# Five small edits to a two-block transformer kernel: zero products, modulation sums, a reordered norm, a join, low parts

## The chip, the cores and the metric

The kernel runs on one core of one Trainium2 chip. The time is that of one execution on the device, in microseconds (us); the number to compare is the median of several runs.

## The reference, cut to what matters

Two blocks of two layers each run over 512 tokens with 1024 features, one after the other, all in fp32.

```
for layer in range(2):                                # first block
    sh1, sc1, g1, sh2, sc2, g2 = split(silu(c) @ ada_w[layer] + ada_b[layer], 6)
    h = rms_norm(x, norm_mix_g[layer]) * (1 + sc1) + sh1
    mix = (RG-LRU and stick-breaking attention)(h) if layer == 0 else (sliding window, sinks)(h)
    x = x + g1 * mix
    h = rms_norm(x, norm_ffn_g[layer]) * (1 + sc2) + sh2
    x = x + g2 * conv_ffn(h)
for layer in range(2):                                # second block
    if layer == 0:
        x = x + diff_attention(rms_norm(x, a_norm)) @ a_w_o
    else:
        k, v = split(rms_norm(x, kv_norm) @ kv_w)     # three groups of 16 heads
        q = rms_norm(x, b_norm) @ b_w_q
        o, lse = [attention with dilation 1, 4, 16 for each group]
        x = x + sum(softmax(lse) * o) @ b_w_o
    x = x + square(relu(rms_norm(x, m_norm[layer]) @ m_w_up[layer])) @ m_w_down[layer]
```

The six modulation vectors of a layer come from one product of a vector with a 1024x6144 matrix. In the dilated attention a query of the group with dilation 4 or 16 sees tokens that lie 4 or 16 apart.

## The kernel before

The residual `x` lies in SBUF with features on partitions: eight chunks `xs[k]` of 128 features by 512 tokens. Every weight product is made of three fp32r products: weights and activations are each split into a high part (a cast) and a low part (the value less its high part), and high x high, low x high and high x low are added up in PSUM. So a chunk of normalised activations takes three steps: the scaled value `t` on VectorE, its high part on ScalarE, its low part on VectorE. A product of a unit takes all eight chunks.

The program isn't written in the order in which it runs. Generators yield operations to a list scheduler (`Flow`) that keeps a clock of its own, has a queue with priorities for each engine, and lets an operation go when its engine is free in the model and its inputs are there. `P_LO` (-1) stands ahead of `P_SECOND` and `P_CRIT` (0), and these ahead of the attention (`P_ATT`, 5). The outcome is one fixed order of instructions for each engine. Buffers are counted in pools ("a": 33 large ones of 4 KB a partition, "t": 14 temporaries); a task waits until it is granted one.

The places that the change touches:

- `layer0_in`, the start. The first chunks come by DMA with their weights; the modulation of layer 0 is made on TensorE in between. Six PSUM banks hold the sums of the first weights. Since two halves of a bank are summed in turn, each bank is first set to zero by a product with a tile of zeros `z` (a memset on GpSimd), as the first thing on TensorE.
- `ada_finish`, the modulation of layer 1. VectorE makes partial sums in the background (`ada_fold`, into `adap`); when a segment is complete, four small products with `sel4` collect the sums of 32 partitions, on TensorE, with the priority `P_CRIT`. It happens three times.
- `h_chunk` makes the normalised chunk of one half of the tokens (256 each), `h_perm` the same for the dilated layer with tokens in another order. The low part of the second half has `P_SECOND`, the one of the first half `P_LO`.
- `layer3`, the dilated attention. For its group 0 the tokens lie in the order "b r j" (blocks of 128, inside them by the remainder r of 4), made in `in3`; groups 1 and 2 need the order "r b j" over all tokens. `second` makes these chunks (`x2`) with `h_perm` after the last unit of group 0, and the buffers of the old order (`x`) come free when all units of group 0 are through. `units` runs a product in two passes of 256 tokens, each pass with two tiles of 128 tokens over all eight chunks.
- `join` adds the weighted outputs of two groups and writes them in the order "b r j"; so the product with `b_w_o` comes out in that order, and `residual` adds it to `xs` through a view that goes through the tokens in steps of four (`perm`).

Of the kernel before, what the change touches and what calls it, by code (L numbers as in the profile page):

```python
# [16 lines left out]
P = 128  # L17
# [191 lines left out]
def body(ctx, tc, I, out, upto=8):  # L209
# [25 lines left out]
    def tmp(n=S):  # L235
        return mk("t", (P, n))
# [106 lines left out]
    one1 = const("one1", (P, 1))  # L343
    adap = const("adap", (P, 192))
# [180 lines left out]

    def proj_tm(u, x, tpair, kinds=()):
        ps = yield from getps(*kinds)
        for t in range(2):
            o = ps[:, t * 256 : (t + 1) * 256]
            tok = slice((2 * tpair + t) * P, (2 * tpair + t + 1) * P)  # L530
            for k in range(8):
                yield x.ready[k][tpair]
                hh, hl = x.h(k)[:, tok], x.l(k)[:, tok]
                wh, wl = u.w(k, slice(0, 256))
                yield mm(3 * fr(256), (o, hh, wh, k == 0, False), (o, hh, wl, False, False), (o, hl, wh, False, k == 7))
        return ps
# [51 lines left out]
    def h_chunk(x, k, hf, r, g, sh=None):  # L588
# [5 lines left out]
        if sh is None:  # L594
            yield acopy(hi, t)
            yield tt(lo, t, hi.bitcast(F32), ALU.subtract, prio=P_SECOND if hf else P_LO)
        else:
            yield act(hi, t, AF.Identity, bias=sh[:, k : k + 1])
            yield stt(lo, t, sh[:, k : k + 1], hi.bitcast(F32), ALU.add, ALU.subtract, prio=P_SECOND if hf else P_LO)
# [158 lines left out]
    def ada_finish(l, segs):  # L758
        s0, n = segs[0], 8 * len(segs)
        if l == 0:  # L760
# [4 lines left out]
            return  # L765
        yield ("pt", 1)
# [225 lines left out]
    def setup():  # L992
# [6 lines left out]
        yield vcopy(silu32[:, :, 0:1], silu_c.unsqueeze(2))  # L999

# [91 lines left out]
    def layer0_in():  # L1092
# [43 lines left out]
        yield ("t", 1)  # L1136
        z = tmp()
        G.memset(z, 0.0)
        for kind in ("pj", "pj", "pj", "ps", "ps", "po"):
            ps = yield from getps(kind)  # L1140
            pss.append(ps)

            yield mm(f4(S), (ps, z[:, :P], z, True, False))
        put("t")
        for k in range(KC):
            yield fr[k]
            yield x.ready[k][0]
            hi, lo = fw[k]
            for m in range(3):
# [485 lines left out]
    def h_perm(x, k, order, ready, h0=0, h1=2):  # L1635
# [10 lines left out]
        yield tt(x.l(k)[:, sl], t, x.h(k)[:, sl].bitcast(F32), ALU.subtract, prio=P_SECOND if h0 else P_LO)  # L1646
# [14 lines left out]
    def layer3(x, tabs):  # L1661
# [102 lines left out]
        def join(o0, o1, y, c, fin):  # L1764
# [3 lines left out]
            yield tt(ta.rearrange("p (b r j) -> p b r j", b=4, r=4), o0[:, c].rearrange("p (b r j) -> p b r j", b=4, r=4),  # L1768
# [38 lines left out]
        for hq in range(4):  # L1807
            three = unit(0, hq, "k"), unit(0, hq, "q"), unit(0, hq, "v")
            k, q, v = yield from (units(x, *three) if hq == 0 else singly(x, three))
# [6 lines left out]
        x.free()  # L1816
        put("rp", 4)
        x2_begun = spawn(second(), P_CRIT)
# [4 lines left out]
        for hq in range(4):  # L1823
            o0, md0, p0, e0 = pre0[hq]
            t = []
            for g in (1, 2):
                for e in tab1 + tab2 * (g - 1):
                    yield e
                k = yield from units(x, unit(g, hq, "k"))
# [10 lines left out]
        yield from out_quarters("bwo", ys, made, perm=True)  # L1840
# [254 lines left out]
```

## Time and profile before

| | us |
|---|---|
| median of 3 runs (2805.18 to 2805.73) | 2805.64 |
| the profiled execution | 2801.65 |
| its span, first to last instruction | 2799.9 |
| TensorE busy (matmul) | 2735.3 |
| VectorE busy | 1777.9 |
| ScalarE busy | 1239.8 |

The span is 1.75 us shorter than the execution that it belongs to. TensorE is near to always busy, so the time is the sum of its products at the clock granted, and of its waits. Line numbers (L304) are those of helpers: every product has L304, every transpose L310, VectorE's tensor_tensor L262, scalar_tensor_tensor L265, ScalarE's activation L292 and copy L295. Names are those of tile pools: a large buffers, t temporaries, b PSUM banks, x the residual.

### The profile page before, as it was taken

What the parts mean: (1) busy time and instruction counts of PE and PEld (TensorE: products, weight loads), DVE (VectorE), ACT (ScalarE), POOL (GpSimd) and SP (SyncE); (2) the same over time, 40 slices, a digit from 0 to 9 for tenths busy, and PEclk for the clock granted to TensorE, in tenths of its full rate; (3) what the DMA queues carried; (4) which work ended last, traced back from release to release, by engine and by line L of the source; (5) the groups of instructions that cost most, each with busy time, mean ns of one, the idle gap of its engine ahead of it and who ended that gap; (6) DMA issues with size and microseconds to landing.
All of it is one profiled execution on the core that took longest, in us unless ns stands there. A gap on an engine that the chain in (4) does not pass through costs nothing.

```text
span 2799.9 us, 43737 instructions
## 1 busy us (share of the span) xinstructions
PE 2735.3 (98%) x17298; PEld 2381.3 (85%) x17298; DVE 1777.9 (63%) x4114; ACT 1239.8 (44%) x2634; POOL 6.4 (0%) x57
## 2 busy tenths in 40 slices
PE   9999999999989999999999999999999999899999
PEld 7777987889869888899988888889899999788888
DVE  5678986457886444588795333676767767943333
ACT  4684423235744232356553322466656554433221
POOL 0000000000000000000000000000000000000000
PEclk9999999999989999999999999999999999999999
DMA  8335564331112223221222223221112123122331
GB/s 306 103 136 218 190 227 148 103 108 61 62 53 91 90 99 112 91 76 46 84 75 84 98 93 103 99 76 61 65 65 76 60 70 97 63 76 91 105 105 62
DMA packets 80270, 281.90 MB, mean 101 GB/s; under 512 B 8896, under 2 KB 11712, under 8 KB 80064
## 3 DMA queue, kind: packets, MB, share of 16 engines
q1 hardware_dynamic: 80064, 279.10, 29.6%
q8 instruction: 136, 2.23, 0.3%
q14 instruction: 70, 0.57, 0.1%
HBM read 276.97 MB, written 2.10 MB: 100 GB/s over the span
## 4 chain that ended last, share of the span: by engine, by line
PE 87%; DVE 9%; ACT 2%; issue 1%; DMA 1%; SPq 0%; ACTq 0%; DVEq 0%
PE b L304 83%; PE b L310 4%; DVE t L262 2%; DVE t L265 2%; DVE a L262 2%; DVE x L262 1%; DVE x L265 1%; DVE a L265 1%; ACT t L292 1%; DMA a<-in_ada_dram 1%; ACT a L295 0%; ACT L220 0%; DVE t L270 0%; DVE s L262 0%; ACT t L295 0%
## 5 line engine op out<-in xcount | busy, mean ns | idle before, releaser
L304 PE MATMUL b<-a,a 128*128 128x256 f32 (+3 forms) x15024 | 2549.0, 332 | 28.8 <-DVE a L262 14.1
L304 PEld LDWEIGHTS b<-a,a 128*128 128x128 f32 (+1 forms) x15024 | 2199.9, 191 | 316.3 <-issue 38.1
L295 ACT CAST a<-a 128x1024 fp32r<-128x1024 f32 (+2 forms) x354 | 357.0, 1035 | 324.5 <-DVE a L262 199.7
L262 DVE TENSOR_TENSOR a<-a,a 128x1024 fp32r<-128x1024 f32 (+2 forms) x362 | 428.8, 1196 | 28.3 <-ACT a L295 20.1
L292 ACT ACTIVATE t<-b 128x512 f32<-128x512 f32 x150 | 88.9, 598 | 313.7 <-PE b L304 312.6
L262 DVE TENSOR_TENSOR x<-b,x 128x512 f32<-128x512 f32 (+1 forms) x144 | 81.8, 573 | 204.2 <-PE b L304 203.6
L295 ACT COPY t<-b 128x512 f32<-128x512 f32 (+3 forms) x194 | 101.2, 524 | 214.9 <-PE b L304 148.0
L265 DVE SCALAR_TENSOR_TENSOR x<-b,mod,x 128x256 f32<-128x256 f32 (+1 forms) x176 | 104.5, 604 | 114.9 <-PE b L304 114.6
L265 DVE SCALAR_TENSOR_TENSOR a<-a,vec,a 128x256 fp32r<-128x256 f32 x288 | 133.1, 483 | 39.4 <-ACT a L292 38.9
L310 PE MATMUL b<-ident,t 128*128 128x128 f32 x896 | 141.3, 278 | 7.6 <-ACT t L295 2.6
L273 DVE CAST a<-t 128x512 fp32r<-128x512 f32 x64 | 27.4, 428 | 190.4 <-ACT t L292 190.4
L295 ACT COPY a<-b 128x512 f32<-128x512 f32 (+1 forms) x146 | 78.1, 537 | 145.1 <-PE b L304 95.9
L292 ACT ACTIVATE a<-a,vec 128x256 fp32r<-128x256 f32 x288 | 132.1, 501 | 0.6 <-DMA a<-in_kvw_dram 0.4
L310 PEld LDWEIGHTS b<-ident,t 128*128 128x128 f32 x896 | 103.0, 141 | 34.0 <-issue 14.1
L292 ACT ACTIVATE t<-t,s,s 128x256 f32<-128x256 f32 (+3 forms) x192 | 113.4, 593 | 28.4 <-DVE s L265 28.4
L292 ACT ACTIVATE t<-t 128x512 f32<-128x512 f32 x108 | 67.6, 633 | 122.7 <-DVE t L265 121.0
L262 DVE TENSOR_TENSOR t<-t,t 128x256 f32<-128x256 f32 (+5 forms) x201 | 105.3, 530 | 13.8 <-ACT t L292 12.2
L276 DVE TENSOR_REDUCE s<-t 128x8 f32<-128x512 f32 (+1 forms) x84 | 56.7, 675 | 85.5 <-ACT t L292 84.9
L262 DVE TENSOR_TENSOR a<-t,a 128x512 fp32r<-128x512 f32 (+1 forms) x188 | 108.0, 601 | 4.2 <-ACT a L295 1.1
L292 ACT ACTIVATE t<-x 128x256 f32<-128x256 f32 (+1 forms) x120 | 51.5, 431 | 118.5 <-DVE x L265 57.1
L295 ACT CAST a<-t 128x256 fp32r<-128x256 f32 (+1 forms) x124 | 62.6, 510 | 90.4 <-DVE t L262 82.5
L262 DVE TENSOR_TENSOR t<-b,rp 128x256 f32<-128x256 f32 x256 | 94.0, 417 | 0.0
(111 smaller groups left out, 1401.7 us busy)
## 6 DMA issues: line engine op xcount, KB each, us to landing
a<-in_ada_dram SPq DMA_DIRECT2D x96, 512.0 KB, 5.3
a<-in_gu_dram SPq DMA_DIRECT2D x88, 512.0 KB, 4.5
a<-in_mu_dram SPq DMA_DIRECT2D x64, 512.0 KB, 4.1
a<-in_md_dram SPq DMA_DIRECT2D x64, 512.0 KB, 3.8
a<-in_kvw_dram SPq DMA_DIRECT2D x48, 512.0 KB, 3.9
a<-in_dn_dram SPq DMA_DIRECT2D x44, 512.0 KB, 3.8
a<-in_aqkv_dram SPq DMA_DIRECT2D x24, 512.0 KB, 4.0
a<-in_bwq_dram SPq DMA_DIRECT2D x24, 512.0 KB, 4.0
```

The lines of the kernel that those rows point to most:

```text
L262: return Op("V", ve(size(o)), lambda: V.tensor_tensor(o, a, b, op), prio=prio)
L265: return Op("V", ve(size(o)) + ptr(sc), lambda: V.scalar_tensor_tensor(o, a, sc, b, op0, op1), prio=prio)
L273: return Op("V", ve(size(o), fast), lambda: V.tensor_copy(o, a))
L276: return Op("V", ve(size(a)), lambda: V.tensor_reduce(o, a, AX.X, ALU.add))
L292: return Op("A", c, lambda: A.activation(o, a, f, scale=scale, **kw), tab=SET_OF.get(f.name), prio=prio)
L295: return Op("A", 0.83e-3 * size(o) + 0.07, lambda: A.copy(o, a), prio=prio)
L304: T.matmul(o, l, r, start=st, stop=sp)
L310: T.transpose(o, a, ident)
```

## The change

1. Start: the zero products become products of fp32r with a constant tile of zeros `zr`, and stand right ahead of the first chunk's products.
2. `ada_finish` waits for 15 us of the scheduler's clock before the sums of layer 1 are collected.
3. The last unit of group 0 (v) and the first one of the new order (k) go chunk by chunk over both passes (`units_k`), on banks that a zero product has set; the v unit gives back the old chunks two at a time, and `second` begins ahead of it.
4. `join` writes in the order of time, and the residual of `b_w_o` is added plainly.
5. The low part of a second half has the priority `P_LO`, too.

```diff
+    zr = const("zr", (P, P), F32R)
...
+    def zeros(ps, r):
+        return mm(fr(S), (ps, zr, r, True, False))
+
+    def units_k(x, u, release=False):
+        yield from u.begin()
+        w = yield from take(u.key)
+        pss = []
+        for tp in range(2):
+            pss.append((yield from getps(*ANY)))
+        for k in range(8):
+            for tp in range(2):
+                yield x.ready[k][tp]
+                if k == 0:
+                    yield zeros(pss[tp], x.h(0))
+                for t in range(2):
+                    o = pss[tp][:, t * 256 : (t + 1) * 256]
+                    tok = slice((2 * tp + t) * P, (2 * tp + t + 1) * P)
+                    hh, hl = x.h(k)[:, tok], x.l(k)[:, tok]
+                    wh, wl = w.w(k, slice(0, 256))
+                    yield mm(3 * fr(256), (o, hh, wh, False, False), (o, hh, wl, False, False), (o, hl, wh, False, k == 7 and t == 1))
+            if release and k % 2:
+                put("a", 2)
+        w.free()
+        for tp in range(2):
+            spawn(u.fin(pss[tp], tp), P_FIN)
+        return u.dst
...
-            yield tt(lo, t, hi.bitcast(F32), ALU.subtract, prio=P_SECOND if hf else P_LO)
+            yield tt(lo, t, hi.bitcast(F32), ALU.subtract, prio=P_LO)
...
+        late = ev()
+        fl.at(fl.now + 15.0, late.set)
+        yield late
         yield ("pt", 1)
         ps = bank()
         yield mm(1.0, *[(ps[:, :n], sel4[:, i, :], adap[...
...
+        yield ts(zr, ones, 0.0, None, ALU.mult)
...
-        yield ("t", 1)
-        z = tmp()
-        G.memset(z, 0.0)
         for kind in ("pj", "pj", "pj", "ps", "ps", "po"):
-            ps = yield from getps(kind)
-            pss.append(ps)
-            yield mm(f4(S), (ps, z[:, :P], z, True, False))
-        put("t")
+            pss.append((yield from getps(kind)))
         for k in range(KC):
             yield fr[k]
             yield x.ready[k][0]
             hi, lo = fw[k]
+            if k == 0:
+                for ps in pss:
+                    yield zeros(ps, hi[:, :S])
...
-            yield tt(ta.rearrange("p (b r j) -> p b r j", b=4, r=4), o0[:, c].rearrange("p (b r j) -> p b r j", b=4, r=4),
+            yield tt(ta.rearrange("p (b j r) -> p b r j", b=4, r=4), o0[:, c].rearrange("p (b r j) -> p b r j", b=4, r=4),
                      o1[:, c].rearrange("p (r b j) -> p b r j", b=4, r=4), ALU.add)
...
-            k, q, v = yield from (units(x, *three) if hq == 0 else singly(x, three))
+            if hq < 3:
+                k, q, v = yield from (units(x, *three) if hq == 0 else singly(x, three))
+            else:
+                k, q = yield from singly(x, three[:2])
+                x2_begun = spawn(second(), P_CRIT)
+                v = yield from units_k(x, three[2], True)
...
-        x.free()
         put("rp", 4)
-        x2_begun = spawn(second(), P_CRIT)
...
-                k = yield from units(x, unit(g, hq, "k"))
+                k = yield from (units_k if g == 1 and hq == 0 else units)(x, unit(g, hq, "k"))
...
-        yield from out_quarters("bwo", ys, made, perm=True)
+        yield from out_quarters("bwo", ys, made)
```

TensorE, the start of the program, before: the zero products (t_113 is the tile of zeros; b_115 to b_162 are the six banks), the first modulation products (with silu), a norm's sum (ones), and the first product of the first chunk (a_125, a_105).

```order
L304 MATMUL b_115<-t_113 128x512
L304 MATMUL b_143<-t_113 128x512
L304 MATMUL b_145<-t_113 128x512
L304 MATMUL b_150<-t_113 128x512
L304 MATMUL b_153<-t_113 128x512
L304 MATMUL b_162<-t_113 128x512
L304 MATMUL b_194<-a_131,silu_88 32x256 x4
...
L304 MATMUL b_262<-a_138,silu_88 32x256 x4
L304 MATMUL b_115<-a_125,a_105 128x256
```

The same engine and place in the changed kernel (b_114 to b_119 are the banks, a_128 and a_106 the first chunk).

```order
L304 MATMUL b_188<-a_134,silu_88 32x256 x4
...
L304 MATMUL b_256<-a_141,silu_88 32x256 x4
L304 MATMUL b_114<-a_128,zr 128x512
L304 MATMUL b_115<-a_128,zr 128x512
L304 MATMUL b_116<-a_128,zr 128x512
L304 MATMUL b_117<-a_128,zr 128x512
L304 MATMUL b_118<-a_128,zr 128x512
L304 MATMUL b_256<-one_89,t_270 128x1 x2
L304 MATMUL b_119<-a_128,zr 128x512
L304 MATMUL b_114<-a_128,a_106 128x256
```

The six zero products have moved from the head of the row to the first product that needs them.

TensorE in the feed-forward of layer 0, before: the third group of modulation sums (adap, sel) behind the last products of one weight unit.

```order
L304 MATMUL b_4395<-a_2592,a_4243 128x512
L304 MATMUL b_4395<-a_2591,a_4244 128x512
L304 MATMUL b_4444<-adap,sel_85 128x16 x4
L304 MATMUL b_4445<-a_2585,a_4230 128x512
L304 MATMUL b_4445<-a_2586,a_4230 128x512
```

In the changed kernel the row behind that unit (b_4394) is at once a product (b_4443), and the sums stand in a later unit.

```order
L304 MATMUL b_4394<-a_2592,a_4245 128x512
L304 MATMUL b_4394<-a_2591,a_4246 128x512
L304 MATMUL b_4443<-a_2585,a_4220 128x512
...
L304 MATMUL b_4548<-a_2585,a_4404 128x512
L304 MATMUL b_4563<-adap,sel_85 128x16 x4
L304 MATMUL b_4548<-a_2585,a_4403 128x512
```

The sums have moved from row 2132 of TensorE's order to row 2207; all rows between are products of 128x512.

VectorE at the change of token order, before: the last small operation of a norm (s_19324), low parts of weights (with vec), and then the chunks in the new order (t<-x,rstd, four-dimensional views) with their low parts.

```order
L269 TENSOR_SCALAR s_19324<-s_19324 128x8
L265 SCALAR_TENSOR_TENSOR a_19335<-a_19333,vec,a_19334 128x256
L265 SCALAR_TENSOR_TENSOR a_19331<-a_19329,vec,a_19330 128x256
...
L262 TENSOR_TENSOR t_19495<-x,rstd 128x4x4x32
L262 TENSOR_TENSOR t_19497<-x,rstd 128x4x4x32
L262 TENSOR_TENSOR t_19498<-x,rstd 128x4x4x32
L262 TENSOR_TENSOR a_19479<-t_19495,a_19478 128x512
```

In the changed kernel the chunks (t_19339 and on) stand ahead of that norm (which has the names s_19323 to s_19326 here) and of those weights.

```order
L269 TENSOR_SCALAR s_19237<-s_19237 128x8
L262 TENSOR_TENSOR t_19339<-x,rstd 128x4x4x32
L262 TENSOR_TENSOR t_19340<-x,rstd 128x4x4x32
L262 TENSOR_TENSOR t_19341<-x,rstd 128x4x4x32
L262 TENSOR_TENSOR a_19329<-t_19339,a_19328 128x512
...
L262 TENSOR_TENSOR t_19342<-x,rstd 128x4x4x32
L276 TENSOR_REDUCE s_19324<-t_19321 128x8
L262 TENSOR_TENSOR t_19322<-b_19231,rp_14461 128x256
```

The eight chunks have moved ahead of the last RoPE and norm of group 0, which now stand between them, and of the weight parts for the v unit's successor.

## Rows read from the trace of the kernel before

**Rows 1.** page, span and part 1: busy us (share of the span) and instructions

```profile
span 2799.9 us, 43737 instructions
...
PE 2735.3 (98%) x17298; PEld 2381.3 (85%) x17298; DVE 1777.9 (63%) x4114; ACT 1239.8 (44%) x2634; POOL 6.4 (0%) x57
```

**Rows 2.** page, part 4: shares of the chain that ended last

```profile
PE 87%; DVE 9%; ACT 2%; issue 1%; DMA 1%; SPq 0%; ACTq 0%; DVEq 0%
```

**Rows 3.** timeline of PE, the start: start, us, engine, operation, [idle before <-releaser]

```profile
1.30 7.73 PE L304 MATMUL b<-t 128*128 128x512 f32 x12 [1.30 <-POOL t L1138]
12.23 0.64 PE L304 MATMUL b<-a,silu 128*32 128x256 f32 x8 [3.20 <-DMA a<-in_ada_dram]
...
23.32 3.22 PE L304 MATMUL b<-a,a 128*128 128x256 f32 x12
```

**Rows 4.** stretches: length, busy us (instructions) of each engine, PEclk, DMA share, GB/s

```profile
12.80:26.50 13.70, 11.72 (x68) 6.83 (x64) 11.92 (x40) 6.33 (x11) 0.00 (x0) 0.50 1.03 409
439.48:446.31 6.83, 5.70 (x17) 4.84 (x18) 6.45 (x11) 2.67 (x4) 0.10 (x2) 0.50 0.40 144
446.40:450.00 3.60, 3.60 (x17) 2.93 (x16) 0.22 (x1) 1.57 (x2) 0.10 (x1) 1.00 0.00 0
2000.40:2016.50 16.10, 10.43 (x43) 8.05 (x42) 15.37 (x36) 8.41 (x20) 0.00 (x0) 0.68 0.19 65
2396.60:2449.90 53.30, 42.74 (x303) 39.51 (x304) 52.12 (x113) 22.16 (x51) 0.00 (x0) 0.97 0.18 60
2446.50:2453.40 6.90, 5.16 (x22) 4.98 (x23) 3.49 (x6) 0.89 (x2) 0.00 (x0) 0.51 0.21 71
```

**Rows 5.** timeline of PE, around the third modulation sums

```profile
440.61 1.89 PE L304 MATMUL b<-adap,sel 128*128 128x16 f32 x8 [3.31 <-DVE adap L276]
```

**Rows 6.** timeline of PE, the change of token order

```profile
2000.98 0.50 PE L304 MATMUL b<-a,a 128*128 128x256 f32 x2 [0.54 <-ACT a L295]
...
2004.53 0.50 PE L304 MATMUL b<-a,a 128*128 128x256 f32 x2 [1.24 <-ACT a L295]
```

**Rows 7.** timeline of DVE ahead of the change of token order

```profile
1986.98 0.17 DVE L269 TENSOR_SCALAR s<-s 128x8 f32<-128x8 f32 x1
```

**Rows 8.** groups by shape of DVE, 1985 to 2017 us: xcount | busy, mean ns

```profile
L262 DVE TENSOR_TENSOR t<-x,rstd 128x512 f32<-128x512 f32 x8 | 8.3, 1077 | 0.0
L262 DVE TENSOR_TENSOR a<-t,a 128x512 fp32r<-128x512 f32 x8 | 5.2, 686 | 1.1 <-ACT a L295 1.1
```

**Rows 9.** groups by shape of DVE, whole span: residual adds and joins

```profile
L262 DVE TENSOR_TENSOR x<-b,x 128x512 f32<-128x512 f32 x80 | 55.3, 692 | 185.0 <-PE b L304 184.4
...
L262 DVE TENSOR_TENSOR x<-b,x 128x256 f32<-128x256 f32 x64 | 26.5, 425 | 19.3 <-PE b L304 19.2
...
L262 DVE TENSOR_TENSOR x<-x,b 128x256 f32<-128x256 f32 x32 | 19.4, 645 | 0.0
...
L262 DVE TENSOR_TENSOR x<-x,b 128x512 f32<-128x512 f32 x16 | 17.4, 1087 | 3.1 <-PE b L304 3.0
...
L262 DVE TENSOR_TENSOR t<-a,a 128x512 f32<-128x512 f32 x8 | 5.4, 694 | 0.0
```

**Rows 10.** timeline of PE, from the last joins to the MLP

```profile
2405.45 0.66 PE L310 MATMUL b<-ident,t 128*128 128x128 f32 x4 [1.81 <-ACT t L295]
...
2408.07 1.19 PE L310 MATMUL b<-ident,t 128*128 128x128 f32 x8 [0.57 <-ACT t L295]
...
2417.09 10.93 PE L304 MATMUL b<-a,a 128*128 128x256 f32 x89 [1.02 <-DVE a L262]
2429.78 0.67 PE L304 MATMUL b<-t,ones 128*128 128x256 f32 x2 [1.76 <-DVE t L262]
...
2437.42 6.13 PE L304 MATMUL b<-a,a 128*128 128x256 f32 x49 [0.70 <-DVE a L262]
2448.24 3.79 PE L304 MATMUL b<-a,a 128*128 128x256 f32 x16 [4.69 <-DVE a L262]
```

**Rows 11.** timeline of PE, second half of layer 1's input

```profile
664.18 5.50 PE L304 MATMUL b<-a,a 128*128 128x256 f32 x31 [2.12 <-DVE a L265]
```

More of the change, by code (lines that the diff above doesn't have):

```diff
@@ L595, in h_chunk @@
             yield acopy(hi, t)
-            yield tt(lo, t, hi.bitcast(F32), ALU.subtract, prio=P_SECOND if hf else P_LO)
+            yield tt(lo, t, hi.bitcast(F32), ALU.subtract, prio=P_LO)
         else:
             yield act(hi, t, AF.Identity, bias=sh[:, k : k + 1])
-            yield stt(lo, t, sh[:, k : k + 1], hi.bitcast(F32), ALU.add, ALU.subtract, prio=P_SECOND if hf else P_LO)
+            yield stt(lo, t, sh[:, k : k + 1], hi.bitcast(F32), ALU.add, ALU.subtract, prio=P_LO)
         put("t")
@@ L1645, in h_perm @@
         yield acopy(x.h(k)[:, sl], t)
-        yield tt(x.l(k)[:, sl], t, x.h(k)[:, sl].bitcast(F32), ALU.subtract, prio=P_SECOND if h0 else P_LO)
+        yield tt(x.l(k)[:, sl], t, x.h(k)[:, sl].bitcast(F32), ALU.subtract, prio=P_LO)
         put("t")
```

## The prediction

> **What bounds the kernel now.** I read the page first. TensorE is busy for 2735.3 of 2799.9 us [rows 1], and the chain that ended last lies on it for 87%, on VectorE for 9% [rows 2]. So the work of other engines costs nothing unless TensorE waits for it, and a product fewer is worth its own step. What can be won is two things: the holes in TensorE's row, and the stretches in which its clock is granted at the lower level. The timeline of TensorE gives the holes with what ended them; the view by stretches gives the clock. [Rows 4] have four stretches with a granted clock of 0.50 to 0.68, each behind or around a hole (the start, 439 us, 2000 us, 2446 us), and for comparison one right behind the second, where the clock is 1.00. Seventeen products of 128x512 take 3.60 us there, 0.212 us each. Products of 128x256 step at 0.125 us at full clock (49 in 6.13 us, the row at 2437.42 in [rows 10]).
>
> **Zero products at the first chunk.** Before, six zero products run from 1.30 us as 12 records, while nothing else can run: TensorE then stands for 3.20 us until a DMA lands at 12.23 us [rows 3]. Taking them away there saves nothing, since the DMA covers them whole. The six now stand ahead of the first chunk's twelve products, which before start at 23.32 us and take 3.22 us (0.27 us each) in the stretch whose clock is 0.50 [rows 3, 4]. At that clock a zero product costs twice 0.212 us, the six 2.5 us. But the twelve are pushed past 26.5 us, where the clock rose: zeros until 25.8, three products at 0.27 us, nine at 0.125 us, done at 27.7 instead of 26.5. I take **+1.1 us**. Bounds: 0, if a later wait for data swallows it, and +2.5, if the clock rises later by as much.
>
> **Late modulation sums.** At 440.61 us TensorE has waited 3.31 us for VectorE's sums (adap), then runs eight small products, and the clock is 0.50 from 439.48 to 446.31 [rows 4, 5]. The program's order shows these products 75 rows later, behind 74 or 75 products of 128x512: 75 x 0.212 = 15.9 us. VectorE's reduction ended right before 440.6 us, and TensorE would now ask at 437.3 + 15.9 = 453.2 us, so the wait has 12 us of cover. What stands behind the eight on TensorE are products that need none of them, and the modulation is read only by layer 1, whose second half is at 664 us [rows 11]. Gain: 3.31 us idle, and of the 5.70 us of TensorE's work at half clock, half, 2.85. The two ends are -3.3 (another hole lowers the clock all the same) and -6.2; this hole is gone altogether and I see none that takes its place, so I take **-6.0 us**. The two earlier groups of sums move likewise and wait for nothing before.
>
> **Chunk-wise change of token order.** From 2000.44 to 2016.5 us TensorE stutters: [rows 6] are two of the eight waits, in turn for ScalarE's cast and VectorE's low part of the permuted chunks. One chunk costs VectorE 1.077 + 0.686 = 1.76 us [rows 8] where TensorE's first pass uses it in three products, 0.38 us, and the clock falls to 0.68 [rows 4]. 43 products in 16.1 us are worth 43 x 0.125 = 5.4 us, so the stage loses 10.7 us. After, the permutations stand on VectorE right behind the small operation that ended at 1987.1 [rows 7], ahead of the last unit's v products instead of behind them. Can they be done in time? Eight chunks are 14.1 us of VectorE, and some 3 us of other rows lie between: the last low part is there at about 2004.5. Their buffers come from the old order's chunks, two at a time; the v unit (96 products, 12.0 us, ended at 2000.4 before) now goes chunk by chunk and frees the first pair 24 products after 1988.4, at 1991.4, the second at 1994.4, before VectorE has done four chunks. The new unit also takes its first products chunk by chunk, 12 products or 1.5 us each: it asks for chunk c at about 2001.3 + 1.5c, the last at 2011.8. VectorE is ahead by 7 us at the last chunk, 10 at the first. Four zero products are added: 4 x 0.212 = 0.85 us. **-10.7 + 0.85 = -9.9 us**. If the next unit's RoPE or weights, now behind the permutations on VectorE, are late instead, half of the loss may come back: -4.9 is the other end. What is moved on TensorE is the attention of the last group of heads, 200 products later, and nothing reads it before the joins.
>
> **Join in the order of time.** VectorE's row order stays; forms change. A residual add through the permuted view takes 1.087 us for 128x512 and 0.645 us for 128x256, the plain one 0.692 and 0.425 [rows 9]: 0.395 us less sixteen times, 0.220 us less 32 times. It counts only where TensorE waits for VectorE, and from 2396 us on it does: VectorE is busy for 52.12 of 53.30 us up to 2450 [rows 4]. The waits are [rows 10]. Ahead of the one at 2405.45 lie four of the long adds: 1.58 of its 1.81 us go. Between it and 2417.09 lie three long and eight short ones (2.9 us), which covers 0.57 and 1.02 us; ahead of 2429.78 lie sixteen short ones, 3.5 us, which covers 1.76. There VectorE has to wait for the product with ones, and what is saved beyond is lost. Nine more short adds (2.0 us) stand before 2448.2: 0.70 us go at 2437.42, and 1.2 of the 4.69 at 2448.24, where TensorE still waits 3.5 us for the low part of the first weights of the MLP. Sum: 1.58 + 0.57 + 1.02 + 1.76 + 0.70 + 1.2 = **-6.8 us**. Against it stands the join's write, now with a step of four elements: eight operations of 0.694 us. Nothing in the trace strides in the write alone; plain costs 0.694, strided in read and write 1.087, so 0 to 3.1 us in all, of which two operations (0 to 0.8 us) lie in this stretch, inside the surplus of 2.9 over 1.59 us. The other six lie where VectorE has pauses. I reckon with the strided price, and it does not change the sum. Of the half-clock stretch at 2446.5 (5.16 us of work, 2.6 lost [rows 4]) I count nothing back: -9.4 is the end with it, -3.4 the end at which every second wait is held by something else.
>
> The Trainium skill speaks here against the change: "SBUF — State Buffer", section "Door 1: The DMA port swizzle", says that each access that crosses into a new 16-byte line pays a penalty, and four fp32 are such a line. The rows of the permuted residual agree (1.087 against 0.692 us). By it the eight joins would cost about 3.1 us more (an estimate, from the price of those rows), though no row here strides in the write alone.
>
> **Low parts first.** In the second half of seven stages VectorE now makes three scaled chunks and then their low parts, instead of eight and eight. Only one of these places shows a wait, 2.12 us at 664.18 [rows 11]. The first chunk is there 2.5 us earlier, but the last one at the same time or 0.6 us later, since VectorE's total is the same, and TensorE uses chunks faster than it gets them. **0**, between -1.5 (the lower clock there is avoided) and +1.
>
> **Sum.** Against the profiled execution (2801.65 us, 1.75 outside its span): 2801.65 + 1.1 - 6.0 - 9.9 - 6.8 = 2780.05. The median of the runs is 3.99 us above that execution, so **2784 us**, 0.77% faster. The ends of the terms add up to 2779 (0, -6.2, -9.9, -9.4, -1.5) and 2798 (+2.5, -3.3, -4.9, -3.4, +1).
>
> **Rivals.**
> - *The wait at 2000 us comes back further on.* RoPE and weight parts of the next units stand behind 14.1 us of permutations on VectorE. For it: VectorE is busy for 15.37 of 16.10 us there [rows 4]. Against it: 7 us of slack by the sums above. With -4.9 for -9.9: 2789 us. 15 in 100.
> - *The end stretch gives its gain back at 2448 us.* If the MLP's weights, not the adds, set that wait, what is won before makes it longer: 4.69 + 3 us or so, and -6.8 becomes -3.4: 2787.5 us. Speaks for it: the wait is for a low part of weights. Against: that operation is queued behind nine adds. 10 in 100.
> - *The late sums do nothing.* If VectorE's lag rather than the sums is what TensorE ran into, it stops at the next product that needs weights: 0 for -6.0, 2790 us. Against: the products that follow run without a hole. 8 in 100.
> - *The clock at the start stays low: slower.* Without the early zeros TensorE's first product comes at 12.23 us. Every microsecond spent at the lower level does half the work, so the loss is half of the time by which the rise comes after 26.5 us. With the rise at 69.7 us all that is won, 21.6 us, is gone; with a rise after 81 us the kernel is slower by over 0.2%, the bound of what a measurement of it can tell from no change; with one at 100 us it takes 2821 us. Against it: before, the clock was at 0.50 from 12.8 to 26.5 us in spite of the early zeros, and rose while TensorE ran the first chunk's products (23.32 to 26.54 us [rows 3]); it runs them, and the zeros ahead of them, after as well. 4 in 100.
>
> The Trainium skill ("TensorE: Matmul & The Clock Gate", Part 1) says that the array starts at the lower clock, is released by work and falls back when idle. The trace agrees that a hole of 3.20 us was followed by 0.50.
>
> **How the numbers follow.** The forecast has 60 in 100, the rivals 37; 3 are left for surprises on either side. Three rivals end at 2787 to 2790 us and two together at 2792 to 2795, the range is 2776 to 2796. By 0.2%, 5.6 us, faster are the forecast, the first three rivals and most of the rest: 0.89. Within it lie combinations of three and a late rise of the clock: 0.06. Slower: 0.05.
>
> **What the profile after would show.** Right: no zero products before 12 us, six at 23 us and the clock 1.00 from about 26.5; no wait at the small products near 450 us and a clock of 1.00 through 437 to 453; between 2000 and 2016 us no row of waits, and some 130 products in 16 us; plain residual adds of 0.69 and 0.43 us, no holes from 2400 to 2437 us but one of 3 to 4 us at the MLP's weights; joins near 1.09 us. Wrong: holes ended by VectorE in the first units after the new order, a clock below 1.00 past 30 us, or a hole over 5 us before the MLP.

## The result, and the profile after

The changed kernel takes 2777.33 us (median of 4 runs, 2776.29 to 2781.52) where the kernel before took 2805.41 in the same comparison (4 runs, 2799.47 to 2805.73): a ratio of 0.9908, with a 95% interval of 0.9891 to 0.9925. A second comparison of the same two kernels gave 0.9919 (0.9907 to 0.9932). It is faster, by 0.8 to 0.9%; the forecast was 2784 us, a ratio of 0.9923. The profiled execution took 2776.29 us.

The page of the changed kernel: the span, part 1 and the shares of the chain, beside [rows 1, 2].

```profile
span 2774.5 us, 43713 instructions
...
PE 2720.7 (98%) x17296; PEld 2374.2 (86%) x17296; DVE 1768.2 (64%) x4115; ACT 1240.0 (45%) x2634; POOL 5.7 (0%) x56
...
PE 89%; DVE 7%; ACT 2%; issue 1%; DMA 0%; SPq 0%; ACTq 0%; DVEq 0%
```

The span is 25.4 us shorter and TensorE is busy for 14.6 us less. Five of these are the zero products at the start (7.73 us in 12 records before, 2.19 + 0.48 in six now). Against that stand four new zero products of the two units that go chunk by chunk; the other products are the same, and fewer of them fell into stretches at the lower clock. VectorE's share of the chain has gone from 9 to 7%.

TensorE's timeline of the changed kernel at the five places, beside [rows 3, 5, 6, 10, 11] (start, us, engine, operation, what ended the idle time before it).

```profile
12.10 2.28 PE L304 MATMUL b<-a,silu 128*32 128x256 f32 x16 [12.10 <-DMA a<-in_ada_dram]
...
22.18 2.19 PE L304 MATMUL b<-a,zr 128*128 128x512 f32 x5
24.99 0.61 PE L304 MATMUL b<-one,t 128*128 128x1 f32 x4 [0.61 <-ACT t L295]
25.46 0.48 PE L304 MATMUL b<-a,zr 128*128 128x512 f32 x1
25.77 0.87 PE L304 MATMUL b<-a,a 128*128 128x256 f32 x6
...
435.75 18.52 PE L304 MATMUL b<-a,a 128*128 128x512 f32 x81
454.11 0.96 PE L304 MATMUL b<-adap,sel 128*128 128x16 f32 x8
...
657.58 1.83 PE L304 MATMUL b<-a,a 128*128 128x256 f32 x9 [0.55 <-ACT a L292]
659.96 0.50 PE L304 MATMUL b<-a,a 128*128 128x256 f32 x2 [0.55 <-ACT a L292]
660.81 1.14 PE L304 MATMUL b<-a,a 128*128 128x256 f32 x7 [0.35 <-DVE a L265]
...
1992.80 0.40 PE L304 MATMUL b<-a,zr 128*128 128x512 f32 x1
1993.04 4.83 PE L304 MATMUL b<-a,a 128*128 128x256 f32 x39
1997.71 0.60 PE L310 MATMUL b<-ident,t 128*128 128x128 f32 x4
1998.06 13.19 PE L304 MATMUL b<-a,a 128*128 128x256 f32 x108
...
2385.96 0.66 PE L310 MATMUL b<-ident,t 128*128 128x128 f32 x4 [0.32 <-ACT t L295]
...
2396.49 10.93 PE L304 MATMUL b<-a,a 128*128 128x256 f32 x89 [0.64 <-DVE a L262]
...
2423.85 3.50 PE L304 MATMUL b<-a,a 128*128 128x256 f32 x16 [3.85 <-DVE a L262]
```

The reader sees all six zero products behind a DMA's landing and not before it (five at 22.18 us, one at 25.46); the modulation sums (454.11) without a wait; three waits of 0.35 to 0.55 us where one of 2.12 us was; the change of token order without any wait; and of the seven waits before the MLP (the six of [rows 10] and one of 0.88 us at 2382) three, of which only the last is large.

VectorE's groups by shape in the changed kernel, beside [rows 9]: residual adds, and the joins (mean ns of one behind the bar).

```profile
L262 DVE TENSOR_TENSOR x<-b,x 128x512 f32<-128x512 f32 x96 | 66.3, 691 | 189.0 <-PE b L304 188.4
...
L262 DVE TENSOR_TENSOR x<-b,x 128x256 f32<-128x256 f32 x96 | 39.2, 424 | 20.1 <-PE b L304 20.0
...
L262 DVE TENSOR_TENSOR t<-a,a 128x512 f32<-128x512 f32 x8 | 8.5, 1103 | 0.0
```

All residual adds cost the plain price, and a join that strides in its write alone costs 1.103 us for 0.694: the strided price of [rows 9] (1.087), to the full.

### The profile page after: what moved, and what is told of

It reads as the page before. It is cut to its first block, busy times and chain, and to the rows that moved or that the text cites. A ratio compares the mean times of both kernels' runs of the same rounds, so it can differ in the third digit from the quotient of the medians.

```text
span 2774.5 us, 43713 instructions
## 1 busy us (share of the span) xinstructions
PE 2720.7 (98%) x17296; PEld 2374.2 (86%) x17296; DVE 1768.2 (64%) x4115; ACT 1240.0 (45%) x2634; POOL 5.7 (0%) x56
## 3 DMA queue, kind: packets, MB, share of 16 engines
q8 instruction: 136, 2.23, 0.3%
## 4 chain that ended last, share of the span: by engine, by line
PE 89%; DVE 7%; ACT 2%; issue 1%; DMA 0%; SPq 0%; ACTq 0%; DVEq 0%
PE b L304 85%; PE b L310 4%; DVE t L262 2%; DVE a L262 1%; DVE t L265 1%; DVE a L265 1%; ACT t L292 1%; DVE x L265 1%; DVE x L262 0%; ACT a L295 0%; DMA a<-in_ada_dram 0%; ACT L220 0%; ACT t L295 0%; DVE s L262 0%; DVE s L276 0%
## 5 line engine op out<-in xcount | busy, mean ns | idle before, releaser
L262 DVE TENSOR_TENSOR x<-b,x 128x512 f32<-128x512 f32 (+1 forms) x192 | 105.5, 557 | 209.1 <-PE b L304 208.3
```

The source lines that it names most:

```text
L262: return Op("V", ve(size(o)), lambda: V.tensor_tensor(o, a, b, op), prio=prio)
```

## The experiments

Each run was profiled, most were also timed against the kernel before on the same chip. Spans alone can't be compared to better than some 5 us, for a reason that the third group of runs shows. So I cut each span at waits that all kernels share, and compare the stretches between: the time from the start of the product behind one wait to that behind the next. They add up to the span. Places are named by their time in the first profiles: "the place near 150 us" is the start of the product behind the wait of 1.95 us there. The last column is the run in which the edit of that stretch is undone.

| stretch (us, in the kernel before) | before, two profiles | changed, two profiles | edit undone |
|---|---|---|---|
| start to 150: zeros | 150.36, 149.30 | 150.69, 155.25 | 149.17 |
| 150 to 279: nothing | 128.93, 129.34 | 128.91, 128.88 | |
| 279 to 655: sums | 375.88, 374.02 | 369.23, 369.24 | 375.46 |
| 655 to 804: low parts | 148.78, 148.85 | 148.03, 148.02 | 148.72 |
| 804 to 1818: nothing | 1013.92, 1013.96 | 1013.98, 1014.05 | |
| 1818 to 1982: low parts | 163.90, 164.31 | 163.13, 163.13 | 164.17 |
| 1982 to 2220: token order (and six joins) | 237.99, 238.11 | 228.33, 228.32 | 238.04 |
| 2220 to 2448: join, residual | 228.48, 229.55 | 221.55, 221.54 | 228.44 |
| 2448 to the end | 351.63, 351.18 | 350.67, 350.67 | 350.86 |

### One edit undone at a time

**Zeros at the start.** The lines of the kernel before in `layer0_in`:

```diff
+        yield ("t", 1)
+        z = tmp()
+        G.memset(z, 0.0)
         for kind in ("pj", "pj", "pj", "ps", "ps", "po"):
-            pss.append((yield from getps(kind)))
+            ps = yield from getps(kind)
+            pss.append(ps)
+            yield mm(f4(S), (ps, z[:, :P], z, True, False))
+        put("t")
...
-            if k == 0:
-                for ps in pss:
-                    yield zeros(ps, hi[:, :S])
```

> The changed kernel with its first edit undone: the six zero products at the head of TensorE's row again, as fp32. The changed kernel's profiled span is 2774.5 us, and its place at the wait near 150 us is 0.3 us later than that of the kernel before. Theory (the zero products cost their time at the lower clock, less what the clock's earlier rise gives back): the clock rises near 26.5 us again, the place near 150 us is back at 150.4, span 2774.2. Rival (something other than the zeros moved the rise of the clock to 23.9 us): the rise stays at 23.9 and the span falls by the price of the zeros at the lower clock, to about 2772.

Measured: span 2774.9 us, ratio 0.9913 (0.9898 to 0.9928), the clock's rise at 24.4 us, the place near 150 at 149.17. Neither holds as put: the place is 1.5 us earlier than in the changed kernel, the span longer. The span's surplus lies elsewhere: from 655 to 804 us this execution took 149.40 us, 1.4 more than the changed kernel with the same program. One profile can't settle a term of a microsecond here; the third group of runs takes all of them together.

**Sums at once.** 

```diff
-        late = ev()
-        fl.at(fl.now + 15.0, late.set)
-        yield late
```

> The changed kernel without the 15 us of delay before the modulation sums. Theory: the wait of 3.3 us for VectorE's sums near 440 us and the stretch of 6.8 us at a clock of 0.50 behind it are back, span 2774.5 + 6.0 to 6.7 = 2780.5 to 2781.2. Rival (the rest of the stage would have been limited by VectorE all the same): the wait is back, but less than half of the time, span under 2777.5.

Measured: span 2783.4 us, ratio 0.9938 (0.9923 to 0.9953). TensorE's timeline of this run, and its stretch view (PEclk is the first number behind the engines):

```profile
443.99 1.89 PE L304 MATMUL b<-adap,sel 128*128 128x16 f32 x8 [3.71 <-DVE adap L276]
```

```profile
442.40:449.10 6.70, 5.11 (x16) 4.43 (x17) 6.35 (x11) 2.67 (x4) 0.20 (x2) 0.50 0.48 159
```

The wait is back, the clock of 0.50 behind it too, and the stretch from 279 to 655 us is 375.46 - 369.23 = 6.2 us longer: the theory holds. The rest of the span's surplus lies ahead of it, where the program is the same (the stretch from 150 to 279 us, 128.9 in the changed kernel, took 131.0 here).

**Token order in passes.**

```diff
-            if hq < 3:
-                k, q, v = yield from (units(x, *three) if hq == 0 else singly(x, three))
-            else:
-                k, q = yield from singly(x, three[:2])
-                x2_begun = spawn(second(), P_CRIT)
-                v = yield from units_k(x, three[2], True)
+            k, q, v = yield from (units(x, *three) if hq == 0 else singly(x, three))
...
+        x.free()
         put("rp", 4)
+        x2_begun = spawn(second(), P_CRIT)
...
-                k = yield from (units_k if g == 1 and hq == 0 else units)(x, unit(g, hq, "k"))
+                k = yield from units(x, unit(g, hq, "k"))
```

> The changed kernel with the token order changed after the last unit of group 0 again, and all units in two passes. Theory: the eight waits and the lower clock near 1993 to 2009 us are back, span 2774.5 + 9.7 = 2784.2. Rival (half of the gain came from elsewhere, or half of the loss was given back further on): span 2779 to 2780.

Measured: span 2787.9 us, ratio 0.9957 (0.9940 to 0.9974). Two of the eight waits that are back, from TensorE's timeline of this run:

```profile
1996.73 0.51 PE L304 MATMUL b<-a,a 128*128 128x256 f32 x2 [0.54 <-ACT a L295]
...
2000.28 0.50 PE L304 MATMUL b<-a,a 128*128 128x256 f32 x2 [1.24 <-ACT a L295]
```

The stretch is 238.04 - 228.33 = 9.7 us longer, as the theory says. Nothing of it was given back further on.

**Only the unit behind it in passes.** Which half of that edit carries the gain: that the permutations begin early, or that the first unit behind them asks for chunks a quarter as fast?

```diff
-                k = yield from (units_k if g == 1 and hq == 0 else units)(x, unit(g, hq, "k"))
+                k = yield from units(x, unit(g, hq, "k"))
```

> The changed kernel with the first unit in the new order (k) in two passes again; the v unit ahead of it still goes chunk by chunk, and the permutations still begin ahead of it. Theory (the early start of the permutations carries the gain): in the changed kernel VectorE ends the last low part at 1994.7 us, where a first pass from 1992.1 us on would ask for it at 1994.7, so at most 1.5 us are lost and two zero products are saved: span 2774.0 to 2775.6. Rival (the chunk-wise pass carries it, since it asks a quarter as fast): waits of 4 us or more and a lower clock near 1995 us, span 2779.

Measured: span 2776.2 us, ratio 0.9916 (0.9899 to 0.9932). TensorE's timeline of this run where the new order begins:

```profile
1985.73 11.80 PE L304 MATMUL b<-a,a 128*128 128x256 f32 x98
1997.37 0.60 PE L310 MATMUL b<-ident,t 128*128 128x128 f32 x4
...
2003.69 0.81 PE L310 MATMUL b<-ident,t 128*128 128x128 f32 x3 [0.40 <-ACT t L292]
```

No wait for a chunk; the stretch is 229.14 us, 0.8 longer than with the chunk-wise unit. The span lies 0.6 us above the theory's range, but behind 2424 us, where the program is the same, this run was 1.2 us longer. The early start carries some 9 of the 9.7 us. The rival falls. The early start and the v unit's chunk-wise order, which gives back the buffers for it, were not run apart.

**Join in blocks.**

```diff
-            yield tt(ta.rearrange("p (b j r) -> p b r j", b=4, r=4), o0...
+            yield tt(ta.rearrange("p (b r j) -> p b r j", b=4, r=4), o0...
...
-        yield from out_quarters("bwo", ys, made)
+        yield from out_quarters("bwo", ys, made, perm=True)
```

> The changed kernel with the join in the order of blocks and the permuted residual add. Theory (VectorE's adds set TensorE's waits in the last part before the MLP): the waits of the kernel before at the same places are back, span 2774.5 + 7 for the waits + 1 for the longer stretch at the lower clock = 2782.5, joins at 0.69 us again, plain adds only elsewhere. Rival (the wait for the MLP's weights gives most of it back): span 2777 to 2778.

Measured: span 2783.7 us, ratio 0.9945 (0.9930 to 0.9960). TensorE's timeline of this run:

```profile
2390.04 0.66 PE L310 MATMUL b<-ident,t 128*128 128x128 f32 x4 [1.90 <-ACT t L295]
...
2414.35 0.67 PE L304 MATMUL b<-t,ones 128*128 128x256 f32 x2 [1.77 <-DVE t L262]
...
2432.80 3.69 PE L304 MATMUL b<-a,a 128*128 128x256 f32 x16 [4.69 <-DVE a L262]
```

The waits of [rows 10] are back to 0.1 us, and the stretch is 228.44 - 221.55 = 6.9 us longer. From 1982 to 2220 us, where the first two of the eight joins lie, this run is shorter, 227.74 for 228.33 us. Two small waits of the changed kernel, each behind a pair of joins, are in neither this run nor the kernel before:

```profile
2126.66 0.66 PE L310 MATMUL b<-ident,t 128*128 128x128 f32 x4 [0.37 <-DVE t L262]
...
2309.39 0.63 PE L310 MATMUL b<-ident,t 128*128 128x128 f32 x4 [0.47 <-DVE t L262]
```

(TensorE's timeline of the changed kernel.) So of the 3.3 us that VectorE spends more on the strided writes, TensorE waits for 0.8. The end behind the MLP's first wait changed by 0.2 us, not by 1.

**Low parts of second halves later.**

```diff
-            yield tt(lo, t, hi.bitcast(F32), ALU.subtract, prio=P_LO)
+            yield tt(lo, t, hi.bitcast(F32), ALU.subtract, prio=P_SECOND if hf else P_LO)
```

(and the two other low parts alike)

> The changed kernel with the low parts of second halves behind the scaled chunks again. In the changed kernel's trace TensorE is 0.74 us earlier behind layer 1's input (near 660 us) than the two edits before it explain, and 0.7 us behind the input of the dilated layer (1830 to 1975 us). Theory as forecast (VectorE's total sets the end of such a stage): span 2774.5, with a wait of 2.1 us near 657 us. Rival (the lower clock behind that wait is the price): span 2775.2, or 2775.9 if the second place too belongs to this edit.

Measured: span 2777.9 us, ratio 0.9919 (0.9904 to 0.9933). TensorE's timeline of this run at both places:

```profile
659.36 2.86 PE L304 MATMUL b<-a,a 128*128 128x256 f32 x14 [2.12 <-DVE a L265]
...
1825.55 6.42 PE L304 MATMUL b<-a,a 128*128 128x256 f32 x32 [3.49 <-DVE a L265]
```

The stretches are 0.7 and 1.0 us longer, as the second half of the rival says; the rest of the span's surplus lies at the start (152.22 us for 150.69). At the first place the clock is the price, as the rival has it: it was at the lower level for 3.4 us behind the wait here and not in the changed kernel's two profiles (more on this below).

### Weights ahead of other work

The largest waits left are for low parts of weights. The first of two tries lets all weights of the next unit go ahead of residual adds and norm steps.

```diff
-        soon = lambda: P_SOON if u.at <= taken[0] else P_W
+        soon = lambda: -0.5 if u.at <= taken[0] else P_W
```

> The changed kernel with one number changed: weights of the next unit to be used go ahead of residual adds and norm steps (priority -0.5 for 0.5). Theory (the wait of 3.85 us at 2423.9 us is for a low part of weights that stands behind such work): that wait falls under 2.5 us and the half-clock stretch behind it goes, and the waits for weights at 279.6 and 648.8 us shrink: span 2769 to 2772. Rival (what is put back is waited for instead, since VectorE works without a pause there): span within 2 us of 2774.5, or longer by up to 5 us.

Measured: span 2776.8 us, ratio 0.9901 (0.9886 to 0.9915). TensorE's timeline of this run before the MLP:

```profile
2396.98 0.62 PE L304 MATMUL b<-a,a 128*128 128x256 f32 x3 [2.23 <-DVE a L262]
...
2423.89 2.54 PE L304 MATMUL b<-a,a 128*128 128x256 f32 x19 [0.98 <-DVE a L262]
2428.23 0.70 PE L304 MATMUL b<-t,ones 128*128 128x256 f32 x2 [1.80 <-DVE t L262]
```

There the rival holds: the wait of 3.85 us shrinks to 0.98, and 2.23 and 1.80 us stand ahead of it and behind; the span is 2.3 us longer. But from the wait near 1811 to the transposes near 1974 us this run was 159.55 us long for 163.13. So the second try does it only for the weights with a gain, those of the dilated layer.

```diff
-        soon = lambda: P_SOON if u.at <= taken[0] else P_W
+        soon = lambda: (P_SOON if u.gain is None else -0.5) if u.at <= taken[0] else P_W
```

> The changed kernel, with the weights that are scaled by a gain (those of the dilated layer) ahead of norm steps, when their unit is next (priority -0.5 for 0.5; other weights as they were). Theory (the wait of 2.8 us near 1822.7 us is for the low part of such weights, which stands behind low parts of the second half; in the run with all weights so, the stretch from the wait near 1811 to the transposes near 1974 us got 3.6 us shorter): the same here, and nothing else moves, span 2774.5 - 3.6 = 2771 give or take 2 us of the clock's difference. Rival (the transposes at 1829 wait for the same VectorE rows, so the gain is given back at once): no difference.

Measured: span 2775.0 us, 2776.79 us (median of 5) where the changed kernel on the same chip took 2780.79; ratio 0.9901 (0.9886 to 0.9915) for 0.9919 (0.9907 to 0.9932). TensorE's timeline of the changed kernel at this place, and then of this run:

```profile
1810.84 0.70 PE L304 MATMUL b<-t,ones 128*128 128x256 f32 x2 [1.45 <-DVE t L262]
...
1822.72 6.30 PE L304 MATMUL b<-a,a 128*128 128x256 f32 x38 [2.80 <-DVE a L265]
1829.33 1.09 PE L310 MATMUL b<-ident,t 128*128 128x128 f32 x8 [0.31 <-DVE t L262]
```

```profile
1814.77 0.70 PE L304 MATMUL b<-t,ones 128*128 128x256 f32 x2 [1.78 <-DVE t L262]
...
1832.91 1.09 PE L310 MATMUL b<-ident,t 128*128 128x128 f32 x8 [1.26 <-DVE t L262]
```

The wait of 2.80 us is gone, a third of it (0.95 us) is waited for at the transposes instead, and the stretch is 159.55 us again, 3.6 less: the theory holds for the stretch. Some of it is given back just ahead: the wait near 1811 has grown from 1.45 to 1.78 us, and from the wait near 804 on the gain is 3.1 us (1173.98 for 1177.11). The span is no shorter than the changed kernel's in its first profile, since this execution was 3.5 us later at the wait near 804 already; the medians differ by 4.0 us.

### The clock behind a short wait

> The kernel before, profiled once more. In nine profiles so far, kernels with the same program at some place wait there alike to 0.1 us, but the clock behind the same wait was at the lower level in some and not in others (behind the wait of 1.95 us near 151 us in four of nine), and the start up to that wait took 150.4 to 152.3 us with one and the same program. Theory (what the clock does behind a short wait differs from execution to execution): all waits as before to 0.1 us, the stretches at the lower clock elsewhere or of other length, the span within 2795 to 2803. Rival (it belongs to the program): the same stretches to 0.1 us.

> The changed kernel once more, for a tighter ratio and a second profile. Theory (the clock behind waits differs from execution to execution): waits alike, stretches at the lower clock moved, span 2773 to 2779; ratio 0.990 to 0.992. Rival: the same stretches at the lower clock, span 2774.5 to 0.3 us.

Both are the unchanged files. Measured: spans of 2798.6 us (before: 2799.9) and 2779.1 us (changed: 2774.5). Each wait of [rows 5, 6, 10, 11] is there again, to 0.3 us, but for the one of 0.57 us at 2408, ahead of which the clock was low. The clock isn't. In the second profile of the kernel before, the stretch at the lower clock around the modulation sums is 3.4 us long instead of 6.8 and the edit's stretch 374.02 us for 375.88; behind the wait near 2404 a stretch at the lower clock is new. The stretch view of the changed kernel at the start, first and second profile (PEclk is the number behind the engines):

```profile
12.10:24.00 11.90, 11.29 (x63) 5.54 (x63) 10.47 (x38) 5.72 (x10) 0.00 (x0) 1.00 1.03 410
24.00:36.00 12.00, 11.39 (x99) 10.25 (x98) 6.42 (x17) 3.48 (x6) 0.00 (x0) 1.00 1.03 405
```

```profile
12.10:24.00 11.90, 9.56 (x63) 4.20 (x63) 10.47 (x36) 5.72 (x10) 0.00 (x0) 1.00 1.03 410
24.00:36.00 12.00, 11.06 (x59) 9.47 (x60) 6.38 (x16) 3.42 (x6) 0.00 (x0) 0.57 1.02 403
```

(The trace has no clock ahead of its first rise, at 23.9 and at 18.2 us, and the view prints 1.00 for it.) In the second profile TensorE was at the higher level from 18.2 us, was through with five zero products in 1.43 us instead of 2.19, and so met the small product behind them too early:

```profile
20.91 1.43 PE L304 MATMUL b<-a,zr 128*128 128x512 f32 x5
24.94 0.93 PE L304 MATMUL b<-one,t 128*128 128x1 f32 x4 [2.60 <-ACT t L295]
```

It waited 2.60 us for ScalarE there, the clock fell, and stayed at the lower level from 25.1 to 35.3 us: 155.25 us to the place near 150 instead of 150.69. And behind the wait of 1.95 us near 151 us, which every profile has, the clock fell in five of the fourteen profiles (the "sums at once" run among them, below) and not in nine.

```profile
151.80:156.10 4.30, 4.29 (x11) 2.36 (x12) 2.33 (x3) 2.08 (x4) 0.00 (x0) 0.60 0.53 180
```

So the theory holds in the main (the waits repeat to 0.3 us and not to 0.1, and the second span of the changed kernel ends 0.1 us above its range), and the rival falls: the waits belong to the program, the stretches at the lower clock partly to the execution. What a single profile says of an edit is uncertain by what they cost, 1.4 to 2 us at a place.

**Zeros in both places.** The lines of the first experiment kept, and the zero products ahead of the first chunk as well.

> The changed kernel with six zero products at the head of TensorE's row as well as ahead of the first chunk (the first six only add work while a DMA is awaited). Theory A (the clock rises when enough dense work has been done behind the wait of 3 us, whatever came before): the clock falls near 12.8 us and rises at 23.9 as in the changed kernel, span 2774.5. Theory B (what was done before the wait sets when the clock can rise): rise near 26.5 us, span 2775.5 to 2776.

Measured: span 2776.9 us, 2778.71 us; the clock fell at 12.7 and rose only at 29.7 us, the place near 150 at 153.13. Later than both theories say; with the spread above the run decides nothing between them.

**Both improvements.** The run with the gained weights, and the zero products at the start.

> As the run before, with the zero products at the head of TensorE's row. Theory (zeros at the start are covered by the DMA, and late they cost 1.3 to 2.5 us, less what the clock gives back): 1.5 us less than the run before, 2769.5. Rival (the clock's difference between executions hides it): equal to 1 us.

Measured: span 2772.1 us, 2775.58 us (median of 4, 2773.97 to 2776.05), ratio 0.9900 (0.9886 to 0.9914); 1.2 us less than the run without the zeros at the start, which the intervals don't separate. By its median it is the fastest version run: 5.2 us below the changed kernel on the same chip. Over all fourteen profiles but the one with both, the place near 150 us lies at 149.2 to 151.5 us with the zeros at the start (four, mean 150.1) and at 150.4 to 155.3 with the late ones (nine, mean 151.8). So the late zeros are 1.7 us dearer in the mean, but the ranges overlap, and the one comparison of medians (1.2 us) doesn't separate them: a cost is likely, its size is not shown.

## Why the prediction was right

The time lies in the forecast's range, 6.7 us below the forecast. Term by term, by the stretches:

| edit | forecast | measured |
|---|---|---|
| zero products late | +1.1 | +1.7 in the mean of profiles |
| late sums | -6.0 | -4.8 to -6.7 (three stretches with the wait less 369.2) |
| token order | -9.9 | -9.7 (two joins in it) |
| join and residual | -6.8 | -6.9 to -8.0; behind it -0.2 to -1 |
| low parts | 0 | -0.7 (by the clock) and -1.0 |
| sum of the spans | -21.6 | -25.4 (first profiles), -19.5 (second profiles) |

**Zero products.** The place was right, and the size lies within the spread of the profiles; the reason for the size was not quite: I took the clock's rise at 26.5 us for a property of the program, and with one and the same start of the program it was up at 23.5 us in one execution and, after a fall, at 35.3 in another. The rival that the clock stays low past 80 us didn't come, but its sign, a clock below 1.00 past 30 us, was there in the second profile: where the clock was up early, TensorE ran into ScalarE's step and lost it again.

**Late sums.** The eight products came at 454.11 us (forecast: 453.2) without a wait, and nothing took its place. The rival of VectorE's lag falls with the run that undoes the edit.

**Token order.** TensorE asked for the first chunk at 1992.1 us and for the last some 10 us later; VectorE's last low parts ended at 1994.8, as its timeline of the changed kernel shows.

```profile
1993.51 1.29 DVE L262 TENSOR_TENSOR a<-t,a 128x512 fp32r<-128x512 f32 x2
```

The rival (the wait returns further on) falls: no wait over 0.4 us stands in the 230 us behind. What I had not weighed is that the chunk-wise second unit is hardly needed: 0.8 of the 9.7 us.

**Join.** I had 0.23 us left at the first of the waits (measured 0.32), nothing at 2417 (0.64), 3.5 at the MLP's weights (3.85), and the three others gone (they are). So the six waits gave 5.7 us and not 6.8. That the stretch still came out at 6.9 is partly luck: a wait of 0.88 us near 2382, which the sum left out, went as well, against 0.47 us of a new wait near 2309; the other 0.8 us of the stretch are not assigned to any wait. The rival that this last wait gives all back falls. The joins' price, which no row of before showed, is the strided one, as I reckoned; that the first six lie where VectorE has pauses was not quite right, since two pairs of them cost TensorE 0.37 and 0.47 us.

**Low parts.** Here a step failed, though a small one: "Only one of these places shows a wait". The dilated layer's input had one as well, 3.53 us near 1830 in the kernel before. It was ended by a low part of weights, but that stood on VectorE behind all eight low parts of the second half. TensorE's and VectorE's rows of the kernel before, and then VectorE's of the changed kernel:

```profile
1830.47 4.10 PE L304 MATMUL b<-a,a 128*128 128x256 f32 x32 [3.53 <-DVE a L265]
...
1827.23 2.79 DVE L262 TENSOR_TENSOR a<-t,a 128x256 fp32r<-128x256 f32 x8
1829.91 0.51 DVE L265 SCALAR_TENSOR_TENSOR a<-a,vec,a 128x256 fp32r<-128x256 f32 x1
```

```profile
1821.15 1.12 DVE L262 TENSOR_TENSOR t<-x,rstd 128x256 f32<-128x256 f32 x2
1822.19 0.47 DVE L265 SCALAR_TENSOR_TENSOR a<-a,vec,a 128x256 fp32r<-128x256 f32 x1
1822.59 0.75 DVE L262 TENSOR_TENSOR a<-t,a 128x256 fp32r<-128x256 f32 x2
```

The weight's low part (with vec) now has two of them behind it, and TensorE goes on 0.7 us sooner. At layer 1's input the first wait of 2.12 us became three of 0.35 to 0.55. What that is worth depends on the clock. Without the edit it fell behind the wait in three of three profiles, and the stretch from 655 to 804 us took 148.72 to 148.85 us. With the edit it fell in three of ten (the run with all weights ahead left out), and these took 149.40 to 149.53 us; the seven others took 147.98 to 148.04. So with the same clock behind it the edit makes the stage 0.7 us longer, as "at the same time or 0.6 us later" has it, and it gains 0.7 us where the clock stays up, which the lower bound of the term allowed for. That it stays up more often behind shorter waits is what these thirteen profiles suggest; they are few.

**Where the 6.7 us went.** Some 1.7 us are the low parts, as the changed kernel was profiled. For the rest no run names an edit: undone one at a time (zeros by their mean), the edits add up to some -23 us, where the medians of the first comparison lie 28.1 us apart and those of the second 23.4. The forecast was put on the median of the runs shown, 2805.64; in three later comparisons the kernel before had medians of 2801.22, 2804.69 and 2804.18. As ratios, forecast (0.9923) and the two measurements (0.9908 and 0.9919) agree within their intervals. The chances I gave don't add up: the forecast and the first three rivals, all faster by over 0.2%, have 93 in 100 by themselves, and I put 0.89.

## What to carry to other kernels

Cut two traces at waits that both have and compare the stretches between: a single span held several microseconds that belonged to no edit, while most stretches without a difference of clock agreed to 0.1 us. When a wait is named for one operation, read what stood ahead of that operation on its engine; the step to move may be there, as the low parts and the weights with a gain show. Work put into a wait that nothing else can use, as the zero products at the start, costs nothing there; moved out of it, it cost more in the mean here, by an amount that the clock's spread nearly hides.

## What the runs showed of the hardware

Behind one and the same wait of 1.95 us TensorE's clock fell to its lower level (1.2 GHz) in five of fourteen executions and stayed at 2.4 GHz in nine; with one and the same start of the program (nine executions) it first rose at 15.7 to 24.5 us. One such fall cost 1.6 us (130.49 us from 150 to 279 us, for 128.9), two in that stretch, the second behind the waits near 185 us, 2.1 (131.0); at the start the executions differ by up to 4.8 us (150.41 to 155.25 us).

A tensor_tensor of 128x512 fp32 on VectorE that writes with a step of four elements (16 bytes) took 1.103 us, where the one with the same reads and a plain write took 0.694: the same price as with strided reads (1.077) or both (1.087).
